# Allocating the two tiles of normalized activations behind the weight tiles

## The chip, the cores and the metric

The kernel runs on one core of a Trainium2 chip. Its engines are named as in the profile: PE is TensorE, PEld its weight loads, DVE VectorE, ACT ScalarE, POOL GpSimd, SP the engine that issues most of the transfers. The metric is the device time of one execution in microseconds (us), lower is better.

## The reference

Two blocks on 512 tokens of 1,024 features, in float32. The first scales and shifts a normalized input, projects it to six groups of columns, and mixes a pooling branch with a chunked recurrence; the second projects a normalized input again and merges four gated branches. Cut to the part that the change touches, the two large projections:

```python
h = rms_norm(h_res, norm_pre_w) * (1.0 + scale) + shift     # 512 x 1024
z = h @ w_in                                                # 1024 x 6144
...
h = rms_norm_2(x, norm_g)                                   # 512 x 1024
proj = h @ w_in_2                                           # 1024 x 11208
```

## The kernel before

Each float32 operand of a large product is split into a rounded part (H) and the rest (L), and a product is three matmuls: H by H, H by L, L by H. The normalized activations stand on chip for a whole block as two tiles, `HH` (rounded part) and `HL` (rest), each 128 partitions x 8 contraction tiles x 512 tokens. They are written twice in the run: at the start of block 1 and at the start of block 2.

The weights come as a stream of `raw` tiles (three buffers), 1 MB a transfer. `pump` splits each group of 128 x 1024 weights into `whi` (ACT, line 244) and `wlo` (DVE, line 245), three buffers of each. `wget` hands out the next pair, two groups ahead.

Two forms of projection read `HH` and `HL`. `proj` (24 matmuls of 512 columns a group) has the weights stationary and streams `HH` and `HL` past them. `a_items` has slices of `HH` and `HL` stationary and streams the weights. Both go through the helper `mm3`, and every matmul is issued at line 268. In the profile, `bank<-HH,whi` is a matmul whose moving operand is `HH` and whose stationary operand is `whi`; `bank<-whi,HH` is the other way round.

All other data of 128 x 512 stand in 54 `slot` tiles and two wider `span` tiles, which the function `get` hands out as they come free. Once block 1's recurrence is done the two spans are handed out like slots. The branch products (`wb` groups in `wb_item`) and the two output projections (`wout_final`) read slots and spans, and `whi`/`wlo`, but not `HH` or `HL`.

Between two groups of the main stream the driver `run` advances side streams (recurrence heads, attention, top-k), whose matmuls are short and read slots, `CST` (constants, the identity among them) or `ONES`.

All of these tiles come from one pool, `const`, in which every tile has one buffer and keeps its place. Addresses are given out in the order in which tiles are allocated.

Of the kernel before, what the change touches and what calls it, by code (L numbers as in the profile page):

```python
# [11 lines left out]
F32R = mybir.dt.float32r  # L12
# [9 lines left out]
NEG = -1e30  # L22
# [11 lines left out]
GS = 3  # L34
DM = 1

# columns of w_in and w_in_2
C_U, C_GP, C_Q, C_F, C_I, C_GH = 0, 1024, 2048, 3072, 4096, 5120
(P_AU, P_AV, P_AZ, P_BQ, P_BC, P_BQI, P_BKI, P_BWI, P_BZ, P_CB, P_CC, P_CX, P_CZ,
 P_DQ, P_DK, P_DV, P_DF, P_DZ, P_G) = (  # L40
# [2 lines left out]

BRANCHES = (0, 2, 3, 1)

# projections of the forgetting attention, ahead of each convolution group
FOX = (["dq0", "dk0", "dq1", "dk1", "dz0", "dq2", "dk2"], ["dq3", "dk3", "dz1"], ["dz2"], ["dz3"])


def plan():  # L50
    """The weight stream: tiles of [128, 2048], each a list of (name, width)."""

    def gates(n):
        r = []
        for p in range(4):
            r += [f"gt{n}_{2 * p}", f"gt{n}_{2 * p + 1}", f"wb{n}_{p}"]
        return r

    raws = []
    for j in range(4):  # L60
        raws.append([(f"s{2 * j}", 896), (f"s{2 * j + 1}", 896)])
    g = ["q3"] + [f"i0_{j}" for j in range(4)] + [f"g{i}" for i in range(4)]
    g += ["u0", "u1", "u2", "u3", "gp0", "gp1", "gp2", "gp3", "pw0"]
    g += [f"f{i}" for i in range(4, 8)] + [f"q{i}" for i in range(4, 8)]
    g += [f"i1_{j}" for j in range(4)] + ["g4", "g5"]
    g += ORD.split()
    g += [f"wp{h}_{j}" for h in range(2) for j in range(4)]
    g += [f"wh{h}_{j}" for j in range(4) for h in range(2)]
    g += [f"av_{j}" for j in range(4)]
    g += ["ki", "qi0", "qi1", "bc"]  # L70
    for i in range(4):
        g += [f"au{i}", f"az{i}"]
    g += gates(0)
    g += [f"dv_{j}" for j in range(4)]
    for i in range(4):
        g += FOX[i]
        g += [f"cc{i}", f"cx{i}", f"cb{i}", f"cz{i}"]
    g += ["bq0", "bq1", "bq2", "bq3", "bz0", "bz1"] + gates(2) + ["bz2", "bz3"] + gates(3) + gates(1)
    g += [f"w2{h}_{j}" for j in range(4) for h in range(2)]
    g = [(n, 1024) for n in g]  # L80
    tail = [g[i:i + 2] for i in range(0, len(g), 2)]
    for i, (m, s) in enumerate(((0, "a"), (0, "b"), (1, "a"), (1, "b"))):
        tail.insert(GP + GS * i, [(f"adg{m}{s}", 2048)])
    return raws + tail
# [3 lines left out]
def kernel(  # L88
# [19 lines left out]
    def act(o, i, func, **kw):  # L108
        return A.activation(o, i, func, **kw)  # L109

# [1 line left out]
    class Slot:  # L112
        """a [128, 512] tile of a place on chip, as float32 and as its rounded form"""

        def __init__(self, i):
            self.i = i
# [31 lines left out]
    spans = deque(const.tile([128, 768], F32, name=f"span{i}", tag=f"span{i}") for i in range(NSPAN))  # L148
    ratios = [const.tile([128, 128], F32, name=f"ratio{i}") for i in range(2)]
    v_i = [0]  # L150
    HH = const.tile([128, 8, 512], F32R, name="HH")
    HL = const.tile([128, 8, 512], F32R, name="HL")
    PV = const.tile([128, pv.shape[1]], F32, name="PV")
    CST = const.tile([128, 576], F32, name="CST")
    MSK = const.tile([128, msk.shape[1]], I32, name="MSK")
# [23 lines left out]
        st_i[0] += 1  # L179
        return t[:, 0:n]  # L180

# [1 line left out]
    raws = plan()  # L183
    raw_t = [const.tile([128, RAW_W], F32, name=f"raw{i}") for i in range(RAWB)]
    whi = [const.tile([128, 1024], F32R, name=f"whi{i}") for i in range(WB)]
    wlo = [const.tile([128, 1024], F32R, name=f"wlo{i}") for i in range(WB)]
    flat = []
    for r, items in enumerate(raws):
        o = 0
# [5 lines left out]
    n = 0  # L195
# [67 lines left out]
        r = flat[i][1]  # L263
        return raw_t[r % RAWB], r

# [1 line left out]
    def mm(o, l, r, start, stop):  # L267
        T.matmul(o, l, r, start=start, stop=stop)  # L268

# [9 lines left out]
            mm3(b[:], h[:, c], l[:, c], HH[:, k, :], HL[:, k, :], k == 0, k == 7)  # L279

    def rsqrt(y, v):
        """y = 1 / sqrt(v), both [128, n]; v > 0."""
        n = v.shape[1]
        t = small(n)
        V.tensor_scalar(t.bitcast(I32), v.bitcast(I32), 1, None, op0=ALU.logical_shift_right)
        V.tensor_scalar(y.bitcast(I32), t.bitcast(I32), -1, 0x5F3759DF, op0=ALU.mult, op1=ALU.add)
        for _ in range(3):
            V.scalar_tensor_tensor(t, y, -0.5, y, op0=ALU.mult, op1=ALU.mult)
            V.tensor_mul(t, t, v)
            V.scalar_tensor_tensor(y, t, 1.5, y, op0=ALU.add, op1=ALU.mult)  # L290
# [14 lines left out]
                tiles[k] = split_slot(tiles[k])  # L305

    def spread(b, w, src, keep=False):
        """b = w^T src, w of zeros and +-1: two passes are exact"""
        h, l = get(), get()
        split(h.r, l.r, src.f)  # L310
        mm(b[:], w, h.r, True, False)
        mm(b[:], w, l.r, False, True)
        put(h, l)
# [1 line left out]
    def bc(row, n=512):  # L315
        return bass.AP(tensor=rows.tensor, offset=rows.offset + row * 512, ap=[[0, 128], [1, n]])

# [1 line left out]
    def load_x():  # L319
        xs = []  # L320
        for t in range(NT):
# [13 lines left out]
    one = get()  # L335
# [94 lines left out]
    for k in range(8):  # L430
# [36 lines left out]
            order = [(o, p) for p in passes for o in range(7)]  # L467
        for o, (w_, h_, first, last) in order:
            mm(sacc[o][:], w_[:, o * 128:(o + 1) * 128], h_[:, k, :], first and k == 0, last and k == 7)
    # lower bounds: softmax over the one layer, its cumulative sum less its first term  # L470
    lbt, lbr = small(8), small(8)
    V.tensor_sub(lbt, PV[:, PV_LB:PV_LB + 8], PV[:, PV_LB:PV_LB + 8])
    act(lbt, lbt, AF.Exp)
# [5 lines left out]
    startup.close()  # L479

    def acc_cols(acc, srcs, kk0, total):
        """acc += columns of ada_w scaled by silu(c), kk0 the first contraction tile of srcs"""
        w = srcs[0].shape[1]
        for i, src in enumerate(srcs):
            kk = kk0 + i
            c = SC_C[:, kk:kk + 1]
            if kk == 0:
                V.tensor_scalar(acc[:, 0:w], src, c, None, op0=ALU.mult)
            else:
                V.scalar_tensor_tensor(acc[:, 0:w], src, c, acc[:, 0:w], op0=ALU.mult, op1=ALU.add)  # L490
# [1 line left out]
    put(*junk, *cb)  # L492
    facc, qacc = sacc[0:4], sacc[4:7]

# [1 line left out]
    lf, kt, qt, vt, gt = {}, {}, {}, {}, {}  # L496
    mixH, mixP = {}, {}

# [27 lines left out]
        return v[:, :, 0:hf], v[:, :, hf:2 * hf]  # L526

    def level(hf, b, q, k, packed=False):
        """[k e^(r - b) | q e^(b - r)] on the halves of each block, r at the first half's end."""
        m, w = get(), get()  # L530
        nb = 512 // (2 * hf)
        d3 = m.f.rearrange("p (b t) -> p b t", t=2 * hf)
        b3 = b.f.rearrange("p (b t) -> p b t", t=2 * hf)
        V.tensor_sub(d3, b3, b3[:, :, hf - 1:hf].to_broadcast([128, nb, 2 * hf]))
        d0, d1 = halves(m.f, hf)
        w0, w1 = halves(w.f, hf)
        act(w0, d0, AF.Exp, scale=-1.0)
        act(w1, d1, AF.Exp)
        k0, _ = halves(k.f, hf)
        _, q1 = halves(q.f, hf)  # L540
        if packed:
            d0 = m.f[:, 0:256].rearrange("p (b t) -> p b t", t=hf)
            d1 = m.f[:, 256:512].rearrange("p (b t) -> p b t", t=hf)
        V.tensor_mul(d0, w0, k0)
        V.tensor_mul(d1, w1, q1)
        put(w)
        return m
# [4 lines left out]
            mm(bank[:, cs], l.f[:, cs], r.f[:, cs], True, True)  # L552

    def quarters(hf, b, q, k):
        """for blocks of four parts of hf tokens: k e^(r - b), r at the end of its own part, and for
        the distances 1, 2, 3 between parts q e^(b - r), r at the end of the part that far back;
        a block's columns for the three distances follow each other (3, 2 and 1 parts)"""
        kd, v = get(), spans.popleft()
        e = ratios[v_i[0] % 2]
        v_i[0] += 1  # L560
# [41 lines left out]
            off += w  # L602

    def half_mm(bank, l, r):
        """64 columns of l against 64 of r for each chunk, into 64 rows of the bank"""
        for c in range(NT):
            mm(bank[0:64, c * 64:(c + 1) * 64], l(c), r(c), True, True)

# [120 lines left out]
        put(gt[h])  # L729
        mixH[h] = o2  # L730

    # driver: side streams advance between the groups of the main stream
    sides = []
    waiting = deque()

# [44 lines left out]
        return (None, mmf, lambda: evac(hold["b"]))  # L780

    def a_items(prefix, evac):
        """token-major projection to 512 columns: evac(t, bank)"""
        hold = {}
        items = []
        for j in range(4):
# [145 lines left out]
    GN = []  # L932
    XT = {}

    # the order of the stream decides where the gate tiles come
    names = [f[0] for f in flat]
    start = names.index("q3")

# [82 lines left out]
        step_sides(2)  # L1021
    free_slots.extend(range(NSLOT, NSLOT + NSPAN))

    # output projection of block 1, residual, norm of block 2
    def load_row(r):
        row = [get(), get()]
        for h in range(2):
# [4 lines left out]
    xs = load_x()  # L1032

    def wout_final(prefix, src, after):
        """token-major product over eight contraction tiles to 1024 columns; the last four weight
        groups run token tile by token tile, after(t, banks) behind each"""
        presplit(src, range(8))
        bk = [[bget() for _ in range(2)] for _ in range(NT)]
        for j in range(2):
# [12 lines left out]
        w = {}  # L1052
# [18 lines left out]
            put(*src[k])  # L1071

    def rstd(t, scaled, row):
        """1 / rms of a token tile's rows; scaled becomes its product with row"""
        ss2, v, r, u = small(2), small(1), small(1), small(1)
        j = get()
        for h in range(2):
# [42 lines left out]
    wout_final("wh", mixH, after1)  # L1120
    put(*ROW, *GN)

# [1 line left out]
    avt = []  # L1124
    w = {}
    first = ws["next"]
# [90 lines left out]
        put(bsb, wst, *avt)  # L1217

    def qi_evac(hp):
        """the queries of two heads, each with its rounded part and its rest in one half each"""  # L1220
        def ev(b):
            for o in range(2):
                s = get()
# [5 lines left out]
        return ev  # L1229

    def topk():
        """bias [query, key] of the query tiles 1.. : 0 at the 128 best keys, NEG at the others"""
        ki = D["ki"]
        kh, kl = get(), get()
        for o in (0, 64):
# [52 lines left out]
        V.tensor_scalar(p.f[:, 0:n], p.f[:, 0:n], rc, None, op0=ALU.mult)  # L1288

    def attn(ready, pre, logits, soft, val, val3, done):  # L1290
        """four heads of causal attention, query tile by query tile: logits, softmax, transposes of
        the weights and, for pairs of query tiles, the products with the values"""
        units = [(h, j) for h in range(4) for j in range(NT)]
        P, W3, WN, lb_, ob_ = {}, {}, {}, {}, {}
        pre(0)
# [511 lines left out]
```

## Time and profile before

| | |
|---|---|
| median of 3 runs | 1154.63 us (1153.57 to 1154.66) |
| span of the profiled execution, first to last instruction | 1152.6 us |
| PE busy | 1131.6 us (98%) |
| DVE busy | 729.2 us (63%) |
| ACT busy | 613.7 us (53%) |
| POOL busy | 64.6 us (6%) |
| granted TensorE clock, mean | 0.997 of full speed |

The profiled execution has no time of its own beside its span; the median of the runs is 2.0 us above the span. A matmul's duration in the profile is a pipelined one (its end is modelled, and the next one starts before it), so the pace of PE is read from the starts of successive matmuls and not from their durations.

### The profile page before, as it was taken

To read this page: it belongs to the slowest core of one execution; us is meant where nothing else is said; L and a number is where in the kernel's file an instruction comes from. 1 tells how busy PE (TensorE), PEld (TensorE's weight loads), DVE (VectorE), ACT (ScalarE), POOL (GpSimd) and SP (SyncE) were. 2 spreads that over 40 slices of the span, in tenths; PEclk is the share of its full clock that TensorE was granted. 3 is DMA by queue.
4 is the path that set the end of the run, shared out by engine and by line. 5 is a ranking of instruction groups with operands and counts; after the bars stand their busy time and mean duration, and the time that the engine had idled before them with its cause. 6 is when DMAs were issued, how large, how long until landed. Compare 5 with 4: busy or idle time off the path is not lost.

```text
span 1152.6 us, 13802 instructions
## 1 busy us (share of the span) xinstructions
PE 1131.6 (98%) x5253; PEld 922.7 (80%) x5253; DVE 729.2 (63%) x1476; ACT 613.7 (53%) x954; POOL 64.6 (6%) x73
## 2 busy tenths in 40 slices
PE   6999999999999999999999999999999999999997
PEld 5778888888878878788888888888878888888885
DVE  7977788663778557789788356465444555543435
ACT  6595497944677365553422353554455767622323
POOL 1320211101320000000000000000000000000000
PEclk9999999999999999999999999999999999999999
DMA  9734223323112452132232323222222222223201
GB/s 329 279 129 147 81 84 128 110 74 110 42 69 76 145 194 71 49 111 80 73 110 83 110 78 97 101 73 92 100 83 73 74 83 98 76 92 110 90 39 73
DMA packets 25422, 118.54 MB, mean 103 GB/s; under 512 B 2950, under 2 KB 3206, under 8 KB 13964
## 3 DMA queue, kind: packets, MB, share of 16 engines
q1 hardware_dynamic: 24780, 116.61, 28.9%
q10 hardware_dynamic: 576, 1.05, 0.2%
q8 instruction: 41, 0.67, 0.2%
q14 instruction: 25, 0.20, 0.1%
HBM read 115.54 MB, written 2.11 MB: 102 GB/s over the span
## 4 chain that ended last, share of the span: by engine, by line
PE 90%; DVE 4%; DMA 2%; ACT 2%; issue 1%; POOL 1%; SPq 0%; POOLq 0%; ACTq 0%
PE bank L268 88%; DVE slot L426 1%; DMA slot<-in_adw_dram 1%; DMA raw<-in_wts_dram 1%; PE bank L1319 1%; ACT slot L109 1%; ACT L109 1%; DMA slot<-in_x_dram 0%; ACT whi L244 0%; POOL slot L852 0%; DVE slot L1083 0%; PE bank L675 0%; DVE slot L1094 0%; DVE slot L1099 0%; ACT slot L230 0%
## 5 line engine op out<-in xcount | busy, mean ns | idle before, releaser
L268 PE MATMUL bank<-HH,whi 128*128 128x512 f32 x960 | 378.4, 401 | 1.2 <-ACT HH L109 1.2
L268 PE MATMUL bank<-HH,wlo 128*128 128x512 f32 x960 | 374.1, 397 | 0.0
L268 PE MATMUL bank<-HL,whi 128*128 128x512 f32 x960 | 373.4, 397 | 0.0
L244 ACT ACTIVATE whi<-raw 128x1024 fp32r<-128x1024 f32 (+1 forms) x170 | 178.8, 1052 | 305.6 <-PE bank L268 253.8
L245 DVE TENSOR_TENSOR wlo<-raw,whi 128x1024 fp32r<-128x1024 f32 (+1 forms) x170 | 206.4, 1214 | 185.0 <-ACT whi L244 179.1
L268 PEld LDWEIGHTS bank<-HH,wlo 128*128 128x128 f32 x960 | 181.2, 189 | 44.0
L268 PEld LDWEIGHTS bank<-HH,whi 128*128 128x128 f32 x960 | 180.5, 189 | 44.7 <-ACT HH L109 3.9
L268 PEld LDWEIGHTS bank<-HL,whi 128*128 128x128 f32 x960 | 181.2, 189 | 41.4
L109 ACT ACTIVATE slot<-slot 128x512 fp32r<-128x512 f32 (+4 forms) x174 | 97.6, 588 | 115.7 <-DVE slot L1658 26.3
L109 ACT ACTIVATE slot<-bank 128x512 f32<-128x512 f32 (+8 forms) x276 | 127.7, 489 | 46.2 <-DVE slot L294 20.6
L268 PE MATMUL bank<-slot,slot 128*128 128x128 f32 (+5 forms) x753 | 131.3, 317 | 3.4 <-ACT slot L109 3.4
L109 ACT ACT_TABLE_LOAD x103 | 132.1, 1283 | 3.1 <-PEq L1796 0.7
L268 PEld LDWEIGHTS bank<-slot,slot 128*128 128x128 f32 (+2 forms) x753 | 109.0, 186 | 19.3 <-issue 4.5
L268 PE MATMUL bank<-slot,whi 128*128 128x512 f32 x264 | 82.6, 391 | 0.0
L268 PE MATMUL bank<-whi,slot 128*128 128x512 f32 x256 | 81.7, 394 | 0.2 <-ACT slot L109 0.2
L294 DVE TENSOR_TENSOR slot<-slot,slot 128x512 fp32r<-128x512 f32 x71 | 48.2, 686 | 15.4 <-ACT slot L109 12.9
L268 PEld LDWEIGHTS bank<-slot,whi 128*128 128x128 f32 x264 | 49.3, 188 | 10.7
L268 PEld LDWEIGHTS bank<-whi,slot 128*128 128x128 f32 x256 | 48.0, 188 | 10.9 <-ACT slot L109 1.0
L268 PE MATMUL bank<-slot,wlo 128*128 128x512 f32 x136 | 53.2, 391 | 0.0
L268 PE MATMUL bank<-wlo,slot 128*128 128x512 f32 x128 | 49.9, 389 | 0.0
L268 PE MATMUL bank<-whi,HL 128*128 128x512 f32 x120 | 47.9, 399 | 1.3 <-DVE HL L294 1.3
L268 PE MATMUL bank<-whi,HH 128*128 128x512 f32 x120 | 47.6, 396 | 0.3 <-ACT HH L109 0.2
(228 smaller groups left out, 1039.6 us busy)
## 6 DMA issues: line engine op xcount, KB each, us to landing
raw<-in_wts_dram SPq DMA_DIRECT2D x89, 1024.0 KB, 4.8
slot<-in_adw_dram SPq DMA_DIRECT2D x32, 256.0 KB, 6.3
slot<-in_x_dram SPq DMA_DIRECT2D x16, 256.0 KB, 4.2
raw<-in_wts_dram SPq DMA_DIRECT2D x8, 448.0 KB, 6.2
slot<-in_rows_dram SPq DMA_DIRECT2D x11, 256.0 KB, 4.1
out_dram<-slot SPq DMA_DIRECT2D x4, 256.0 KB, 2.5
out_dram<-slot ACTq DMA_DIRECT2D x4, 256.0 KB, 2.3
slot<-CUM SPq DMA_DIRECT2D x3, 256.0 KB, 4.9
```

The source lines that it names most:

```text
L109: return A.activation(o, i, func, **kw)
L244: A.activation(whi[s][:, 0:w], src, AF.Copy)
L245: V.tensor_sub(wlo[s][:, 0:w], src, whi[s][:, 0:w])
L268: T.matmul(o, l, r, start=start, stop=stop)
L294: V.tensor_sub(dst_l, src, dst_h)
L426: V.tensor_tensor_reduce(junk[i % 2].f, ada[k][i].f, cb[i % 2].f, 1.0, 0.0, ALU.mult, ALU.add, mds[k][:, i:i + 1])
L1319: T.transpose(tb[:, cs], P[u1].f[:, cs], IDENT)
```

## The change

The two lines that allocate `HH` and `HL` move from ahead of the constants to behind `raw`, `whi` and `wlo`. No instruction, no order and no wait changes on any engine; the built program differs in on-chip addresses alone. (Comments are taken out as well.)

```diff
     ratios = [const.tile([128, 128], F32, name=f"ratio{i}") for i in range(2)]
     v_i = [0]
-    HH = const.tile([128, 8, 512], F32R, name="HH")
-    HL = const.tile([128, 8, 512], F32R, name="HL")
     PV = const.tile([128, pv.shape[1]], F32, name="PV")
     CST = const.tile([128, 576], F32, name="CST")
...
     raw_t = [const.tile([128, RAW_W], F32, name=f"raw{i}") for i in range(RAWB)]
     whi = [const.tile([128, 1024], F32R, name=f"whi{i}") for i in range(WB)]
     wlo = [const.tile([128, 1024], F32R, name=f"wlo{i}") for i in range(WB)]
+    HH = const.tile([128, 8, 512], F32R, name="HH")
+    HL = const.tile([128, 8, 512], F32R, name="HL")
     flat = []
```

The addresses of the built programs, in bytes within a partition, and what is left when they are divided by 64 and by 512:

| tile | bytes | before | after | left by 64, before and after | left by 512, before and after |
|---|---|---|---|---|---|
| span0, span1 | 3,072 each | 16,512 to 22,656 | the same | 0, 0 | 128, 128 |
| HH | 16,384 | 23,680 | 82,400 | 0, 32 | 128, 480 |
| HL | 16,384 | 40,064 | 98,784 | 0, 32 | 128, 480 |
| CST | 2,304 | 56,704 | 23,936 | 0, 0 | 384, 384 |
| ONES | 512 | 62,080 | 29,312 | 0, 0 | 128, 128 |
| raw0 to raw2 | 8,192 each | 66,016 to 90,592 | 33,248 to 57,824 | 32, 32 | 480, 480 |
| whi0 to whi2 | 4,096 each | 90,592 to 102,880 | 57,824 to 70,112 | 32, 32 | 480, 480 |
| wlo0 to wlo2 | 4,096 each | 102,880 to 115,168 | 70,112 to 82,400 | 32, 32 | 480, 480 |
| slot0 to slot53 | 2,048 each | 115,168 to 225,760 | the same | 32, 32 | 480, 480 |

The tiles that stood behind `HL` and ahead of the slots move down by 32,768 bytes, which leaves their remainders as they were. The slices of `HH`, `HL`, `whi`, `wlo` and the slots that the large products read start at multiples of 512 bytes within their tile, and keep its remainder.

## Rows read from the trace of the kernel before

**Rows 1.** The page: span, PE's busy time, chain that ended last by engine.

```profile
span 1152.6 us, 13802 instructions
PE 1131.6 (98%) x5253; PEld 922.7 (80%) x5253; DVE 729.2 (63%) x1476; ACT 613.7 (53%) x954; POOL 64.6 (6%) x73
...
PE 90%; DVE 4%; DMA 2%; ACT 2%; issue 1%; POOL 1%; SPq 0%; POOLq 0%; ACTq 0%
```

**Rows 2.** Chain that ended last, in time: start us, us, what.

```profile
67.23 0.50 ACT slot L109
67.78 46.70 PE bank L268 x223
...
320.09 0.86 POOL slot L851
...
330.56 33.50 PE bank L268 x161
...
403.77 1.14 ACT slot L230 x2
...
416.16 0.96 PE bank L268 x3
...
445.35 0.69 DVE slot L1094
...
466.43 7.72 PE bank L268 x32
...
1145.22 0.70 DVE slot L1658
```

**Rows 3.** Windows from 68 us: instructions reading HH, then HL.

```profile
68.00:1153.00 1085.00, 662.85 (x2042) 384.59 (x2041) 5.29 (x8) 4.28 (x8) 0.00 (x0) 1.00 0.26 92
...
68.00:1153.00 1085.00, 405.51 (x1021) 192.63 (x1021) 5.29 (x8) 0.00 (x0) 1.00 0.26 92
```

**Rows 4.** Timeline of PE, two `proj` groups: first matmul, and the one behind the 48.

```profile
1017.51 0.40 PE L268 MATMUL bank<-HH,whi 128*128 128x512 f32 x1
...
1028.76 0.63 PE L268 MATMUL bank<-slot,whi 128*128 128x512 f32 x2
```

**Rows 5.** Timeline of PE, `a_items`: nine matmuls apart.

```profile
640.14 0.39 PE L268 MATMUL bank<-whi,HH 128*128 128x512 f32 x1
...
642.24 0.39 PE L268 MATMUL bank<-whi,HH 128*128 128x512 f32 x1
```

**Rows 6.** Timeline of PE, last output projection: twelve matmuls apart.

```profile
1109.64 0.39 PE L268 MATMUL bank<-wlo,slot 128*128 128x512 f32 x1
...
1112.36 0.39 PE L268 MATMUL bank<-wlo,slot 128*128 128x512 f32 x1
```

**Rows 7.** Timeline of PE, a `wb` group on slots: twelve and twelve matmuls apart.

```profile
880.13 0.63 PE L268 MATMUL bank<-slot,whi 128*128 128x512 f32 x2
...
882.89 0.62 PE L268 MATMUL bank<-slot,whi 128*128 128x512 f32 x2
...
885.61 0.74 PE L268 MATMUL bank<-slot,slot 128*128 128x256 f32 x5
```

**Rows 8.** Timeline of PE, another such group: twelve and twelve matmuls apart.

```profile
900.88 0.64 PE L268 MATMUL bank<-slot,whi 128*128 128x512 f32 x2
...
903.67 0.61 PE L268 MATMUL bank<-slot,whi 128*128 128x512 f32 x2
...
906.39 0.84 PE L268 MATMUL bank<-slot,slot 128*128 128x512 f32 x3
```

**Rows 9.** Timeline of PE, a `wb` group with spans: 24 matmuls from first to last.

```profile
590.26 0.63 PE L268 MATMUL bank<-slot,whi 128*128 128x512 f32 x2
...
591.65 0.63 PE L268 MATMUL bank<-span,whi 128*128 128x512 f32 x2
...
595.82 0.40 PE L268 MATMUL bank<-HH,whi 128*128 128x512 f32 x1
```

**Rows 10.** Windows: us, busy PE, PEld, DVE, ACT, POOL, PEclk, DMA share, GB/s.

```profile
475.00:600.00 125.00, 124.97 (x562) 101.57 (x560) 104.82 (x196) 48.81 (x68) 0.00 (x0) 1.00 0.25 87
600.00:800.00 200.00, 200.00 (x922) 163.40 (x921) 112.86 (x243) 87.99 (x149) 0.00 (x0) 1.00 0.29 96
800.00:1100.00 300.00, 300.00 (x1360) 244.51 (x1360) 145.09 (x249) 155.42 (x226) 0.00 (x0) 1.00 0.25 87
```

**Rows 11.** The page, groups by line: products of slots with weights.

```profile
L268 PE MATMUL bank<-slot,whi 128*128 128x512 f32 x264 | 82.6, 391 | 0.0
L268 PE MATMUL bank<-whi,slot 128*128 128x512 f32 x256 | 81.7, 394 | 0.2 <-ACT slot L109 0.2
...
L268 PE MATMUL bank<-slot,wlo 128*128 128x512 f32 x136 | 53.2, 391 | 0.0
L268 PE MATMUL bank<-wlo,slot 128*128 128x512 f32 x128 | 49.9, 389 | 0.0
```

## The prediction

> **What bounds the kernel now.** I read the page first: PE is busy for 98% of the span and holds 90% of the chain that ended last [rows 1]. The chain in order of time then says where PE does not set the end. Up to 67.78 us it runs through transfers, DVE and ACT. After that it leaves PE only in three places worth naming: a pooling chain from 320.09 to 330.56 us, a piece of the last recurrence head from 403.77 to 416.16, and the norm at the end of block 1 from 445.35 to 466.43 [rows 2]; the end of the run from 1145.22 us on, behind the last matmul, is the fourth. Everything else is one matmul after another at line 268.
>
> So the question is the pace of the matmuls. All the large ones have 512 columns and the same form, and differ in what they read. I took the pace from the starts in PE's timeline, in stretches in which PE waits for nothing:
> - `proj`, with `HH` and `HL` moving: 48 matmuls from 1017.51 to 1028.76 us, 234.4 ns each [rows 4].
> - `a_items`, with `HH` and `HL` stationary: 9 matmuls in 2.10 us, 233.3 ns each [rows 5].
> - the output projection, with slots stationary and weights moving: 12 matmuls in 2.72 us, 226.7 ns each [rows 6].
> - a branch product, with slots moving and weights stationary: 12 matmuls in 2.76 us (230.0 ns) and then 12 in 2.72 us (226.7 ns) [rows 7]. A second one has 232.5 ns and then again 226.7 ns [rows 8].
>
> The reader is to see two things. A product of slots with weights comes to 226.7 ns a matmul, after a start of about a dozen slower ones; a product with `HH` or `HL` stays near 234 ns however long it runs. And it does so in either role: moving in [rows 4], stationary in [rows 5]. The granted clock is 1.00 in all these stretches [rows 10], so the clock is not the difference. The shapes are alike, and ACT and DVE split weights beside all of them.
>
> What is left is the place. In the table of addresses, `whi`, `wlo` and every slot leave 32 when divided by 64 (480 by 512); `HH` and `HL` leave 0 (128 by 512). A third witness speaks for the place and against the tiles' role: spans hold the same kind of data as slots and go through the same loop, but leave 0 by 64. The branch group of [rows 9], in which 6 of 24 matmuls read spans, has 5.56 us for 24 matmuls, 231.7 ns each, and does not come down to the pace of [rows 7], whose whole 24 take 5.48 us (228.3 ns).
>
> **The change part by part.** No instruction is added, removed or moved. Of the addresses, those of the weights, constants and small tiles fall by 32,768, which leaves every remainder up to 512 as it was; I cost this at nothing, and bound it below by a rival. `HH` and `HL` get the remainder of the slots and the weights. After the change each of their matmuls has both operands at the remainders of [rows 6 to 8].
>
> The gain from one matmul: 234.1 (between [rows 4] and [rows 5], nearer to [rows 4], which stand for nine in ten) less 226.7 ([rows 6], and the ends of [rows 7, 8]) is 7.4 ns.
>
> How many: from 68 us on, 2,042 matmuls read `HH` and 1,021 read `HL` [rows 3], together 3,063. Those ahead of 68 us stand in the stage that transfers, DVE and ACT bound, and give nothing. 3,063 x 7.4 ns = 22.7 us.
>
> What comes off:
> - The slow start. A stretch needs about a dozen matmuls before it runs at 226.7 ns. The excess of the first twelve is 12 x 3.3 = 40 ns in [rows 7] and 12 x 5.8 = 70 ns in [rows 8], where the first one still holds part of a change from another kind of matmul. I take the start to be paid again whenever short matmuls of a side stream, `CST` or `ONES` come between. 3,063 matmuls are at most 128 groups of 24, of which some follow each other directly; with 95 starts at 30 ns (many start nearer to the pace than these two) that is 2.9 us. Its bounds are 0 and 95 x 70 ns = 6.6 us.
> - Places where the end is not PE's. Of the three chains above, only the one from 320.09 to 330.56 has `proj` groups beside it; 10.5 us of them would have given 10.5 x 7.4 / 234 = 0.3 us. I add 1.0 us as an estimate for side chains that now arrive just ahead of PE and will arrive just behind it; the bound is 4 us. DVE is the engine to watch: from 475 to 600 us it is busy 104.8 of 125 us, 84% [rows 10], and with PE 3% faster it would be at 86%, still short of a bound.
>
> Sum: 22.7 - 2.9 - 1.3 = 18.5 us. The transfers have room for it: their share is 0.25 to 0.29 in these windows [rows 10].
>
> **A rule that speaks against it.** By the rows, a matmul's pace depends on where its operands stand. The Trainium skill's page "TensorE: Matmul & The Clock Gate", in its section "Part 2: What happens when you issue a matmul", says the opposite of what I build on: PE has two independent read ports, so loading the next weights takes no read bandwidth from the running matmul, and the pace is set by the number of columns alone. By that rule the change would be worth nothing and the time would stay at 1154.6 us. The trace does not agree for this form of matmul, with 226.7 against 234.4 ns for the same 512 columns; what in the addresses makes the difference is not shown by it.
>
> **The rivals.**
> 1. Nothing changes (1154.6 us): `HH` and `HL` are slow for something other than their place, such as their length or how they were written. For it: every slow row is one of few tiles. Against it: the spans of [rows 9], which are filled and read by the same code as slots, and that the slowness comes in both roles.
> 2. Slower: not the remainder but the height of the address decides. All slow tiles of before (spans, `HH`, `HL`, `ONES`) stand below 62,592 and all fast ones that PE reads above 90,592, so a line between these would explain the rows too. The change brings `whi` and `wlo` down to 57,824 to 82,400. If the line lies above 82,400, every product with weights has a slow operand: `HH` and `HL` gain nothing, and the 264 + 256 + 136 + 128 = 784 products of slots with weights [rows 11] go from about 227.5 to 234 ns, 784 x 6.5 = 5.1 us more: 1159.7 us. Against it: [rows 4] pass over all of `HH` and `HL`, 32,768 bytes, at one pace, and the slots of [rows 6 to 8] lie anywhere in 110,592 bytes and settle at one pace, so no other line is seen, and this one would have to fall in the one gap.
> 3. The same with a line between 62,592 and 70,112, so that `whi` alone comes below it, in whole or in part. Two of three matmuls then have a slow stationary operand, but groups with a fast buffer gain: at one such buffer of three, a third of 22.7 - 2.9 us is 6.6, less two thirds of the 5.1, which is 3.4, leaves 3.2 us: 1151.4 us. This decides against rival 2 at the point where `wlo` stays above the line.
> 4. The new pace is reached but mostly lost: starts at 70 ns each and waits at 4 us leave 22.7 - 6.6 - 4.3 = 11.8 us: 1142.8 us. I count this as the far end of the forecast.
>
> **How the numbers follow.** The remainder decides, 0.81: span 1152.6 - 18.5 = 1134.1, and with the 2.0 us between span and median 1136.1 us. Its own range is 1130.5 (no starts, no waits, and slots behind `HH` spared their own slow start, another 1.4 us at most) to 1142.8. Rival 1 has 0.08, rival 2 has 0.06, rival 3 has 0.05. A measurement of this kernel can tell about 0.2%, 2.3 us, from no change. Faster by more than that: 0.81 + 0.05 = 0.86. Within it: 0.08. Slower: 0.06. The range of 8 in 10 is the forecast's own, drawn out on the slow side for a pace between the two: 1130.5 to 1146.
>
> **What the profile after would show.** In two undisturbed `proj` groups the 48 matmuls of [rows 4] should take 10.9 us and not 11.25, with a pattern of 226 and 227 ns between starts once it has settled; the `a_items` of [rows 5] should be at 226.7 ns; the output projection and the branch groups without spans should stay as they are in [rows 6 to 8]. If those went to 234 ns, rival 2 or 3 holds. The first 68 us should be alike. PE's waits should grow by about 1 us in all, near 330 us first. The prediction is wrong if the `proj` groups stay at 234 ns, or if they do come down and PE then waits for DVE by more than 4 us.

## The result and the profile after

| | before | after |
|---|---|---|
| median of the runs | 1154.31 us (4 runs, 1153.57 to 1154.66) | 1136.13 us (4 runs, 1133.66 to 1137.48) |
| ratio, 95% interval | | 0.9846 (0.9833 to 0.9859) |
| span of the profiled execution | 1152.6 us | 1134.0 us |
| PE busy | 1131.6 us | 1112.3 us |

The time falls by 18.2 us, 1.5%, and the span by 18.6. Of the busy times on the page of after only PE's moves: it falls by 19.3 us, and the other engines stay within 1 us of what they were.

```profile
span 1134.0 us, 13802 instructions
PE 1112.3 (98%) x5253; PEld 921.7 (81%) x5253; DVE 729.3 (64%) x1476; ACT 613.5 (54%) x954; POOL 64.9 (6%) x73
...
PE 86%; DVE 4%; DMA 3%; ACT 3%; issue 2%; POOL 2%; SPq 0%; POOLq 0%; ACTq 0%
```

The chain that ended last, of after, in order of time (start us, us, what):

```profile
67.24 0.49 ACT slot L109
67.78 45.49 PE bank L268 x223
...
113.75 0.47 PE bank L268 x3
...
153.04 26.83 PE bank L268 x139
...
194.19 1.06 ACT whi L244
...
197.69 86.13 PE bank L268 x418
...
315.29 1.12 POOL slot L851
...
326.02 33.08 PE bank L268 x161
...
440.41 0.69 DVE slot L1094
...
461.49 7.64 PE bank L268 x32
```

Against [rows 2]: nothing up to 67.78 us, then the same 223 matmuls in 45.49 us where 46.70 were needed. At the pooling chain the run is 4.8 us ahead and at the norm 4.9: in between PE waits 0.4 us longer at the pooling chain, the projections behind it gain as much, and the rest are the products of block 1's output, which read slots. From 461.49 us on, the lead grows to the end.

In two stretches the chain leaves PE where that of before did not: from 114.22 to 153.04 us, through ACT, DVE, POOL and time in which the profile shows no wait ("issue"), and from 194.19 to 197.69 us. That is why PE's share of the chain falls from 90% to 86%. PE itself loses little there: the step up to the matmul at 153.04 takes 0.55 us, where the same step of before took 0.29.

Timelines of PE, of after, in the order of [rows 4 to 9]: two `proj` groups (first matmul, and the one behind the 48), `a_items` (nine matmuls apart), the output projection (twelve), two branch groups on slots (twelve and twelve each), and one with spans (24 from first to last).

```profile
1000.90 0.39 PE L268 MATMUL bank<-HH,whi 128*128 128x512 f32 x1
...
1011.78 0.61 PE L268 MATMUL bank<-slot,whi 128*128 128x512 f32 x2
...
625.05 0.39 PE L268 MATMUL bank<-whi,HH 128*128 128x512 f32 x1
...
627.09 0.39 PE L268 MATMUL bank<-whi,HH 128*128 128x512 f32 x1
...
1087.70 0.39 PE L268 MATMUL bank<-wlo,slot 128*128 128x512 f32 x1
...
1090.42 0.39 PE L268 MATMUL bank<-wlo,slot 128*128 128x512 f32 x1
...
865.77 0.63 PE L268 MATMUL bank<-slot,whi 128*128 128x512 f32 x2
...
868.53 0.62 PE L268 MATMUL bank<-slot,whi 128*128 128x512 f32 x2
...
871.25 0.74 PE L268 MATMUL bank<-slot,slot 128*128 128x256 f32 x5
...
886.18 0.64 PE L268 MATMUL bank<-slot,whi 128*128 128x512 f32 x2
...
888.96 0.61 PE L268 MATMUL bank<-slot,whi 128*128 128x512 f32 x2
...
582.41 0.62 PE L268 MATMUL bank<-slot,whi 128*128 128x512 f32 x2
...
583.77 0.63 PE L268 MATMUL bank<-span,whi 128*128 128x512 f32 x2
...
587.90 0.39 PE L268 MATMUL bank<-HH,whi 128*128 128x512 f32 x1
```

The 48 matmuls take 10.88 us, 226.7 ns each, where [rows 4] have 234.4; the nine of `a_items` take 2.04 us, 226.7 ns, where [rows 5] have 233.3. The output projection has 2.72 us for twelve as in [rows 6], and the branch groups still start slowly, with 2.76 and then 2.72 us as in [rows 7] and 2.78 as against 2.79 in [rows 8]. The group with spans is at 5.49 us (228.8 ns), down from 5.56 in [rows 9]: it now comes from a `proj` group at the fast pace, and its first six matmuls, on slots, take 1.36 us where [rows 9] have 1.39; the pace is lost at the first span. (The windows of [rows 10], from which the prediction has the clock, end at 1100 us; at [rows 6], from 1109 to 1113 us, the granted clock is 1.00 too.)

The pooling chain is where PE's wait grows most. Timeline of PE, of before and then of after, with the idle time ahead of an instruction and what ended it in brackets:

```profile
329.02 1.07 PE L268 MATMUL bank<-slot,ONES 128*128 128x512 f32 x2 [1.36 <-DVE slot L294]
...
324.48 1.08 PE L268 MATMUL bank<-slot,ONES 128*128 128x512 f32 x2 [1.77 <-DVE slot L294]
```

### The profile page after: what moved, and what is told of

The parts are those of the page before. It is cut to its first block, busy times and chain, and to the rows that moved or that the text cites. A ratio compares the mean times of both kernels' runs of the same rounds, so it can differ in the third digit from the quotient of the medians.

```text
span 1134.0 us, 13802 instructions
## 1 busy us (share of the span) xinstructions
PE 1112.3 (98%) x5253; PEld 921.7 (81%) x5253; DVE 729.3 (64%) x1476; ACT 613.5 (54%) x954; POOL 64.9 (6%) x73
## 4 chain that ended last, share of the span: by engine, by line
PE 86%; DVE 4%; DMA 3%; ACT 3%; issue 2%; POOL 2%; SPq 0%; POOLq 0%; ACTq 0%
PE bank L268 84%; DMA slot<-in_adw_dram 2%; ACT slot L109 1%; POOL slot L852 1%; PE bank L1319 1%; ACT L109 1%; ACT whi L244 1%; POOL slot L851 1%; DMA raw<-in_wts_dram 1%; DVE slot L426 1%; DMA slot<-in_x_dram 0%; DVE slot L1083 0%; DVE slot L1094 0%; DVE slot L1099 0%; PE bank L675 0%
## 5 line engine op out<-in xcount | busy, mean ns | idle before, releaser
L268 PE MATMUL bank<-HH,whi 128*128 128x512 f32 x960 | 372.6, 395 | 0.8 <-ACT HH L109 0.6
L268 PE MATMUL bank<-HH,wlo 128*128 128x512 f32 x960 | 368.0, 391 | 0.0
L268 PE MATMUL bank<-HL,whi 128*128 128x512 f32 x960 | 367.1, 390 | 0.0
```

## The experiments

The prediction left open what it is in the address that counts. Each kernel below is the kernel before or the change with padding between tiles; none changes an instruction, an order or a wait. The **distance** in the table is the address of the moving operand less that of the stationary one, in `proj`, as it is left by 256 (why 256, e5 shows). In `a_items` the weights move and `HH` and `HL` are stationary, so there the distance has the other sign. All ratios are against the kernel before, timed beside: its medians were 1153.36 to 1153.71 us beside e1 to e12.

| run | HH at | distance | `proj`, ns a matmul | median us | ratio, 95% interval |
|---|---|---|---|---|---|
| before | 23,680 | 160 | 234.4 | 1154.31 | |
| the change | 82,400 | 0 | 226.7 | 1136.13 | 0.9846 (0.9833 to 0.9859) |
| e11, the change again | 82,400 | 0 | 226.7 | 1135.51 | 0.9841 (0.9828 to 0.9855) |
| e1 | 23,712 | 128 | 233.1 | 1150.92 | 0.9974 (0.9964 to 0.9983) |
| e2 | 82,432 | 32 | 233.3 | 1153.79 | 1.0001 (0.9991 to 1.001) |
| e3 | 23,680 | 128 | 233.1 | 1148.18 | 0.9955 (0.994 to 0.9969) |
| e4 | 82,464 | 0 | 226.7 | 1135.32 | 0.9839 (0.9825 to 0.9854) |
| e8 | 24,032 | 0 | 226.7 | 1135.67 | 0.9843 (0.9829 to 0.9856) |
| e5 | 82,656 | 0 (256 by 512) | 226.7 | 1135.65 | 0.9844 (0.983 to 0.9857) |
| e9 | 82,464 | 64 | 229.4 | 1142.63 | 0.9907 (0.9893 to 0.992) |
| e10 | 82,416 | 16 | 231.7 | 1146.77 | 0.9938 (0.9925 to 0.9952) |
| e7, HL alone | 23,680 | 160, HL 0 | 232.1 | 1149.36 | 0.9962 (0.9948 to 0.9976) |
| e6, all alike | 83,072 | 0 | 226.7 | 1134.54 | 0.9834 (0.9821 to 0.9847) |
| e12, e6 again | 83,072 | 0 | 226.7 | 1134.59 | 0.9831 (0.9817 to 0.9844) |

**Remainder by 64, or height (e1, e2).** In e1 `HH` and `HL` stay low and leave 32 by 64 like all the rest; in e2 they stand behind the weights and leave 0.

```diff
+    padA = const.tile([128, 8], F32, name="padA")
     HH = const.tile([128, 8, 512], F32R, name="HH")
     HL = const.tile([128, 8, 512], F32R, name="HL")
+    padB = const.tile([128, 8], F32, name="padB")
```

> HH and HL stay at their old height (23,712 and 40,096) but leave 32 by 64, like the weights and slots, since 32 bytes of padding stand ahead of and behind them. If the remainder by 64 decides: as the change, 1136 us, proj matmuls 226.7 ns apart. If the height of the address decides (everything below about 57,000 is slow): as before, 1154 us, 234 ns apart.

> HH and HL stand behind the weights as in the change, but 32 bytes further, so that they leave 0 by 64 while weights and slots leave 32. If the remainder decides: as before, 1154 us, 234 ns apart in proj. If the height decides: as the change, 1136 us.

e1 meets neither: a gain of 0.26%, and `proj` at 233.1 ns. Timeline of PE in e1, two `proj` groups of 48 matmuls:

```profile
1014.48 0.40 PE L270 MATMUL bank<-HH,whi 128*128 128x512 f32 x1
...
1025.67 0.63 PE L270 MATMUL bank<-slot,whi 128*128 128x512 f32 x2
```

The same remainder by 64 is not enough. And e2, at the new height, gives all of the change's gain back (in part on the slots, as shown below), so the new height is not enough either. Timeline of PE in e2, the same 48, 233.3 ns each, then twelve matmuls of a branch group on slots behind its first twelve, and twelve of the output projection:

```profile
1016.92 0.40 PE L270 MATMUL bank<-HH,whi 128*128 128x512 f32 x1
...
1028.12 0.62 PE L270 MATMUL bank<-slot,whi 128*128 128x512 f32 x2
...
1030.86 0.62 PE L270 MATMUL bank<-slot,whi 128*128 128x512 f32 x2
...
1033.61 0.40 PE L270 MATMUL bank<-HH,whi 128*128 128x512 f32 x1
...
1100.96 0.63 PE L270 MATMUL bank<-whi,slot 128*128 128x512 f32 x2
...
1103.76 0.63 PE L270 MATMUL bank<-whi,slot 128*128 128x512 f32 x2
```

The padding of e2 has a second effect, which is the strongest sign that the tiles `HH` and `HL` themselves are not the cause. Its slots move up by 64 bytes and its weights do not, so the products of slots with weights come to a distance of 64 where slots move, and of -64 where weights do. Both lose the settled pace of 226.7 ns: the branch group takes 2.75 us for twelve, 229.2 ns each, and the output projection 2.80 us, 233.3 ns each ([rows 6] have 2.72). e9 has `HH` and `HL` at these two distances.

**Absolute or relative (e3, e4).** In e3 the kernel before has 32 bytes of padding ahead of `raw`, so that weights and slots leave 0; in e4 the change has 32 bytes ahead of the spans and again ahead of `raw`.

```diff
+    padA = const.tile([128, 8], F32, name="padA")
     raw_t = [const.tile([128, RAW_W], F32, name=f"raw{i}") for i in range(RAWB)]
```

> HH and HL stand where they stood before; raw, weights and slots move up by 32 bytes, so that every operand of PE leaves 0 by 64, spans, CST and ONES too. If the two operands of PE have to agree (relative remainder): 1136 us or a little less, 1133 to 1136, as rows with spans and ONES join and fewer slow starts are paid. If a remainder of 0 is slow in itself (absolute): all large matmuls stay at or go to 234 ns, also those of slots with weights, 1154 + 5 = 1159 us.

> The change, with 32 bytes of padding ahead of the spans and again ahead of raw: every operand of PE leaves 32 by 64, spans, CST and ONES too. By both forms of the remainder theory the rows with spans (some 55) and ONES (22) come to 226.7 ns, and the slow starts behind them and behind CST are spared: up to 2.9 us under the change, 1133 to 1136 us. If short matmuls break the pace whatever their addresses are: 1135.5 to 1136 us.

e3 meets neither number either, since both theories took the remainder by 64 for the whole of it. But its `proj` runs at the pace of e1, 233.1 ns, and e1 and e3 have the distance of 128 at different remainders: `HH` is at 23,712 against 23,680, and the weights leave 32 by 512 against 0. And its products of slots with weights, which now leave 0, keep their pace. Timeline of PE in e3: the 48 of `proj`, and then in the output projection eight matmuls in 1.81 us, 226 ns each.

```profile
1013.37 0.40 PE L269 MATMUL bank<-HH,whi 128*128 128x512 f32 x1
...
1024.56 0.63 PE L269 MATMUL bank<-slot,whi 128*128 128x512 f32 x2
...
1104.82 0.39 PE L269 MATMUL bank<-whi,slot 128*128 128x512 f32 x1
...
1106.63 0.62 PE L269 MATMUL bank<-whi,slot 128*128 128x512 f32 x2
```

So none of the remainders tried is slow in itself; what goes with the pace is the distance between the two operands. Whether it is a matmul's own stationary operand that counts, or that of the next matmul, whose load overlaps it, these runs don't separate: within a stretch both stand at the same remainder. (That e3 is 2.7 us faster than e1 at the same pace of `proj` stays open; the steps of PE from 67.8 us on, each cut at 245 ns, account for 1.0 us of it.) In e4 the distance in `proj` is 0 as in the change, at other addresses, and the time is that of the change.

**The old place with the right distance (e8), and the period (e5).** In e8 `HH` and `HL` stay ahead of the constants and move up by 352 bytes (the padding of e1 with 352 and 160 bytes); in e5 the change has them 256 bytes further (256 and 256 bytes).

> HH and HL stay ahead of the constants, at 24,032 and 40,416, 352 bytes above their old place, so that they leave 480 by 512, as weights and slots do; 160 bytes of padding behind HL keep all other remainders. If the distance between the two operands of a matmul by 512 decides (0 is fast): as the change, 1136 us. If the low place matters in any way: 1149 to 1154 us, as in the runs whose distance is not 0.

> The change, with HH and HL 256 bytes further, so that they leave 224 by 512 and weights and slots 480: a distance of 256. If the distance counts by 256: fast, 1136 us, proj matmuls 226.7 ns apart. If it counts by 512: 1149 to 1154 us and 232 to 234 ns, as with the distances 32, 128 and 160.

Both are as fast as the change. Timeline of PE in e8, 48 matmuls in 10.88 us, and then the same of e5, 10.88 us:

```profile
1001.06 0.39 PE L270 MATMUL bank<-HH,whi 128*128 128x512 f32 x1
...
1011.94 0.62 PE L270 MATMUL bank<-slot,whi 128*128 128x512 f32 x2
```

```profile
999.02 0.39 PE L270 MATMUL bank<-HH,whi 128*128 128x512 f32 x1
...
1009.90 0.61 PE L270 MATMUL bank<-slot,whi 128*128 128x512 f32 x2
```

e8 shows that it is not the new place that gives the gain: the old one does as well, 352 bytes up. e5 gives the period: 256 counts as 0, 128 does not.

**Other distances (e9, e10).** e9 is the change with `HH` and `HL` 64 bytes further (64 and 192 bytes of padding). In e10 they are read and written 16 bytes into longer tiles (`HL` like `HH`):

```diff
-    HH = const.tile([128, 8, 512], F32R, name="HH")
+    HHw = const.tile([128, 4224], F32R, name="HH")
+    HH = HHw[:, 4:4100].rearrange("p (k n) -> p k n", k=8)
```

> The change, with HH and HL 64 bytes further: a distance of 64 from weights and slots, which agree among themselves by 256. If any distance other than a multiple of 256 bars the settled pace: 1148 to 1154 us, as with 32, 128 and 160. If only some do: between these and 1136 us.

> The change, with HH and HL read and written 16 bytes into a longer tile: a distance of 16. If the two operands have to agree to the byte by 256: 1148 to 1154 us. If a small distance is tolerated: 1136 us.

e9 lies between the two, with 60% of the change's gain left (10.7 of 17.9 us, against e11); e10 keeps 37%, and its time lies just under those expected if the operands have to agree to the byte, because one of its two kinds of projection runs as fast as in the change. In `a_items` the roles are swapped, and with them the sign of the distance. Timeline of PE in e10: the 48 of `proj` at a distance of 16, 231.7 ns, and then 66 matmuls of `a_items` at a distance of -16 in 14.96 us, 226.7 ns each.

```profile
1010.25 0.39 PE L270 MATMUL bank<-HH,whi 128*128 128x512 f32 x1
...
1021.37 0.62 PE L270 MATMUL bank<-slot,whi 128*128 128x512 f32 x2
...
629.87 0.39 PE L270 MATMUL bank<-whi,HH 128*128 128x512 f32 x1
...
644.83 0.39 PE L270 MATMUL bank<-whi,HH 128*128 128x512 f32 x1
```

In e9 it is the other way round: `a_items`, at -64, take 233.2 ns each (63 matmuls from 629.98 to 644.67 us), `proj`, at 64, 229.4 (48 in 11.01 us). Both are within 0.2 ns of the slots of e2 at the same distances.

```profile
629.98 0.39 PE L270 MATMUL bank<-whi,HH 128*128 128x512 f32 x1
...
644.67 0.40 PE L270 MATMUL bank<-whi,HH 128*128 128x512 f32 x1
...
1006.15 0.40 PE L270 MATMUL bank<-HH,whi 128*128 128x512 f32 x1
...
1017.16 0.63 PE L270 MATMUL bank<-slot,whi 128*128 128x512 f32 x2
```

In all these runs the weights are the moving operand at -16 and -64, and the stationary one at 16 and 64. So the runs don't tell whether it is the sign or the role that makes 16 and -16 differ.

**Half of the change (e7).** Only the allocation of `HL` moves.

> Half of the change: HL stands behind the weights at a distance of 0 by 512, HH stays at its old place at a distance of 160. One in three of the proj matmuls, those with HL moving, then has operands that agree. If each matmul is fast or slow by itself: a third of the change's 18 us, 1148 us. If a matmul with other operands ahead of it spoils the pace of the next: 1152 to 1154 us.

4.4 us, a quarter of the change's gain, between the two expectations. `proj` runs at 232.1 ns, 2.3 less than before, which is 30% of the 7.7 that the whole change gives there, where a third would be 2.6. Timeline of PE in e7, the 48 of `proj` in 11.14 us:

```profile
1012.82 0.40 PE L268 MATMUL bank<-HH,whi 128*128 128x512 f32 x1
...
1023.96 0.62 PE L268 MATMUL bank<-slot,whi 128*128 128x512 f32 x2
```

That fits a pace set mostly matmul by matmul, with something spoilt behind a matmul at another distance. The branch groups with spans in the change show how much: behind three matmuls on spans (at a distance of 160) the next three, on slots (at 0), still take 234.1, 231.8 and 228.8 ns from start to start, on the mean of 16 such places, and only the fourth is back at 226.7.

**All operands alike (e6, e12).** Padding ahead of `CST`, `ONES` and `raw` in the change brings spans, constants and `ONES` to the same remainder too.

```diff
+    padA = const.tile([128, 64], F32, name="padA")
     CST = const.tile([128, 576], F32, name="CST")
...
+    padB = const.tile([128, 64], F32, name="padB")
     ONES = const.tile([128, 128], F32R, name="ONES")
...
+    padC = const.tile([128, 40], F32, name="padC")
     raw_t = [const.tile([128, RAW_W], F32, name=f"raw{i}") for i in range(RAWB)]
```

> The change, with padding so that every operand of PE leaves 128 by 512: HH, HL, weights, slots, spans, CST and ONES. If the distance by 512 decides, the rows with spans (some 55) and ONES (22) come to 226.7 ns and no slow start is paid behind them: 1132.5 to 1135 us. If short matmuls break the pace by themselves: 1135.5 to 1136 us.

> The change itself once more, beside the next run on the same chip: 1136 us.

> All operands of PE at 128 by 512 once more. If the rows with spans and ONES are worth what they cost: 0.5 to 2 us under the change. If not: the same.

The median of e6 is 1.6 us under the change's, which was timed apart from it, and that of e12 0.9 us under e11's, which was timed beside it; the intervals overlap both times, so the time cannot tell it from the change. The traces can: with every step of PE from 67.8 us on cut at 245 ns, which takes the waits out, the steps add up to 1043.4 us in the change and in e11, and to 1042.1 us in e6 and in e12. Timeline of PE in e6: the branch group with spans takes 5.44 us for its 24, 226.7 ns each (5.49 in the change); a branch group behind short matmuls still needs 2.76 us for its first twelve and 2.72 for the next.

```profile
582.17 0.62 PE L271 MATMUL bank<-slot,whi 128*128 128x512 f32 x2
...
587.61 0.39 PE L271 MATMUL bank<-HH,whi 128*128 128x512 f32 x1
...
865.32 0.63 PE L271 MATMUL bank<-slot,whi 128*128 128x512 f32 x2
...
868.08 0.62 PE L271 MATMUL bank<-slot,whi 128*128 128x512 f32 x2
...
870.80 0.74 PE L271 MATMUL bank<-slot,slot 128*128 128x256 f32 x5
```

The spans' slowness goes with the distance (the 32 steps behind matmuls with a moving span and stationary weights have a mean of 232.7 ns in the change and 226.8 in e6), so the third witness of the prediction was a good one. The slow start does not: it is still paid in e6, behind short matmuls on `CST` and slots that stand at the same remainder as the rest.

## Why the prediction was right

- **The bound.** PE's pace sets the time, and a faster pace comes out but for 1.2 us. Nothing changed ahead of 67.78 us, and the chain still leaves PE at the three places that were named. It now leaves it in two more, up to 153.04 and up to 197.69 us; the forecast had not named them, but had 1.0 us for side chains that come to arrive just behind PE.
- **The gain of one matmul.** 7.4 ns were taken. In `proj` it was 234.4 - 226.7 = 7.7 and in `a_items` 233.3 - 226.7 = 6.6; nine in ten of the matmuls are of the first kind, which makes 7.6. Nine matmuls are few: over all steps behind the thirteenth of a stretch `a_items` go from 233.2 to 227.3 ns and `proj` from 234.2 to 226.7, which makes 7.3.
- **The count, the starts and the waits.** The forecast had 22.7 - 2.9 = 19.8 us of pace and 1.3 us lost to waits. Added up over PE's timeline from start to start, the steps behind the 3,063 matmuls from 67.8 us on shrink by 18.9 us, and those behind all other matmuls grow by 0.4. With every step cut at 245 ns, which takes the waits out, they shrink by 19.4 and by 0.3, 19.7 us in all. So the pace gave 19.7 us and the waits took 1.2: 0.4 at the pooling chain, where 0.3 had been worked out and PE now waits 1.77 us for DVE and not 1.36, 0.3 at 153 us, 0.2 at 138 us, and 0.3 ahead of four short matmuls between 824 and 845 us. At the settled paces alone, the 2,688 matmuls with `HH` or `HL` moving and the 375 with them stationary would have given 22.4 us, so starts and changes of operands took 3.0 of them, where 2.9 had been estimated.
- **The span.** 18.5 us were forecast, 18.6 came; the time was forecast at 1136.1 us and is 1136.13. That is closer than the parts deserve: starts and waits were estimates, and that both came out within 0.2 us is in part luck.
- **What counts in the address.** The forecast rested on `HH` and `HL` coming to the remainder of the weights, and named it by 64 and by 512 in one breath, first by 64. By 64 it is wrong (e1, e3): it is the distance between the two operands, by 256, and no remainder of its own. The change happens to set that distance to 0, so it was luck that the number did not depend on the reading; a change that had matched the remainders by 64 alone would have been forecast 15 us too fast.
- **The rivals.** Rival 1 falls with the result. Rivals 2 and 3 fall with the rows of after, where products of slots with weights keep 226.7 ns with weights at 57,824 to 82,400, and e8, with the old height and the time of the change, leaves the height no part that can be seen. The rule of the Trainium skill that spoke against the change ("TensorE: Matmul & The Clock Gate", section "Part 2: What happens when you issue a matmul") says that the two read ports are independent and that the number of columns alone sets the pace. For matmuls of this form the second does not hold here: the kernels of the table have the same instructions and differ by up to 7.7 ns a matmul, and what they differ in is how the addresses of the two operands stand to each other. Whether it is the two reads that get into each other's way, against the first, is not shown.

## What to carry to other kernels

Where PE is the bound and streams float32r operands of 512 columns, compare the pace of matmuls of the same form that read different tiles: 3% between them, in every stage and in both roles, was the sign of the addresses here. Then try to give the tiles that PE reads together addresses that agree by 256 bytes. Here a tile or two of padding did it, and what had broken it were small tiles between the large ones. An allocation order is part of a kernel's tuning: in this kernel the size of the small tiles between `HL` and the weights is worth up to 1.5%.

## What had not been expected of the hardware

The settled pace of a 512-column float32r matmul with a weight load each is 226.7 ns here, and it comes with the moving and the stationary operand at the same address by 256 bytes: in `proj` a distance of 16 costs 5.0 ns, 32 costs 6.6, 64 costs 2.7, 128 costs 6.4 and 160 costs 7.7, while in `a_items` -16 costs nothing that can be seen and -64 costs 6.5. So the cost does not simply grow with the distance, and 16 and 64 cost something else than -16 and -64, by the sign or by the role of the weights. That two reads of PE meet somewhere in the on-chip memory would fit, since it depends on PE's own two operands and both roles show it, but that is not shown: no run looked at the memory itself. Why 64 is better than 32 and 128, and why -16 is free, stays open.
